# Seven block products in place of eight in a hybrid layer's mixer projections, with the value projections moved ahead and weight sums made in place

## Chip, cores and metric

The kernel runs on one core of a Trainium2 chip. The metric is device time in microseconds. Engines: PE (TensorE, matrix products), DVE (VectorE), ACT (ScalarE), POOL (GpSimd), SP (which issues nearly all transfers).

## What is computed

One step of an encoder layer on 640 tokens (512 of a prompt, 8 x 16 of samples), model width 1024, all in float32:

```python
x = x + 0.5 * swiglu(rms_norm(x), ffn1_w_in, ffn1_w_out)      # width 2816
z = rms_norm(x) @ w_in_mix     # RQ RK RV RG | FQ FK FV forget | two gates
q, k = rotary(RQ), rotary(RK)
o_ret = rms_norm(retention(q, k, RV)) * silu(RG)              # 4 heads
o_fox = forgetting_attention(norm(FQ), norm(FK), FV, forget)  # 8 heads
x = x + (sigmoid(g0) * (o_ret @ w_br_ret) + sigmoid(g1) * (o_fox @ w_br_fox)) @ w_out
x = x + 0.5 * swiglu(rms_norm(x), ffn2_w_in, ffn2_w_out)
x = x + (p @ w_ple) * sigmoid(rms_norm(x) @ w_ple_gate)
```

States, keys, values and forget logs are outputs too. Samples attend to a cache of 1024 frames.

## The kernel before

**Precision.** Each weight and activation is split in two: a high part, rounded to the matmul's fp32r format (a cast on ACT, L262 for weights), and a low part, the rest (a subtraction on DVE, L263). A product is three matmuls: high x high, high x low, low x high. `Parts` holds split weights; its tiles `wh` and `wl` have 7 slots (`NW`) of 512 columns.

**Feed-forward stages** (first one to about 470 us, second from about 1200 us). Input projections are done two column blocks at a time (gate and up, 128 columns each, `Seven`). Weights of a block are four quarters (two outputs x even and odd slices of 128 input features), the tokens two halves of 320. Seven products of sums (`ORDER`, each 4 slices x 3 matmuls of 320 columns) in three PSUM banks a, b, c replace eight plain ones. `Seven.__init__` and `split` form the sums of weights on DVE (L386 to L388, L395), partly into tiles of their own (`att`); `after` combines the banks (L413 to L421). `Norm.add_pair` makes the sums of activations (t1 to t4) in `sums` (L349 to L353), as high and low parts. Output projections go through `gemm_t`.

**The mixer** (470 to about 1088 us). A list of units, 256 weight columns each, is a feed that `run_units` turns into matmuls a few at a time: kind "n" is token-major (values, fox q and k, the last embedding product), kind "t" feature-major (retention's RQ, RK, RG, the gates, the fox output): two outputs x two halves of 320 tokens, each 8 slices x 3 matmuls into one `pg` bank, then one DVE step (`spill_t`, L753) that scales it, and a store to `zdram`. Units are loaded two ahead and split one ahead. Attention and retention run beside the feed: their steps are emitted by hand, and after each one `fill(us)` lets the feed run for so many us of the kernel's own clock (`mm` charges 320 / 2400 us for a matmul of 320 columns). The constants FILL_P0, FILL_P1 (prompt attention), FILL_S0, FILL_S (samples) and FILL_R (each of 13 steps per retention head) set how much. `defer` queues follow-up steps. `until("rv")` runs the feed as far as the values of retention, then retention starts.

Order of units before: fox v(1), q, k, v(0), q, k; RQ (2 units), RK (2), RV (4), RG (4), gates G1 (4) and G0 (4); embedding (4), fox output (4).

**Buffers.** PSUM: six `pa` banks, two `pg` banks. SBUF tiles of 640 columns: `blk` 35 slots, `att` 8, `tmp` (320 columns) 10; the tile framework orders instructions from these and from the order in which they are written. Each engine runs its queue in order.

Of the kernel before, what the change touches and what calls it, by code (L numbers as in the profile page):

```python
# [19 lines left out]
P = 128  # L20
# [26 lines left out]
FILL_P0, FILL_P1, FILL_S0, FILL_S, FILL_R, FILL_B = 1.76, 1.6, 19.8, 10.0, 3.0, 6.4  # L47
# [84 lines left out]
def kernel(  # L132
# [17 lines left out]
    NBLK, NKV, NATT, NTMP, NRAW, NW, NTINY = 35, 4, 8, 10, 2, 7, 24  # L150
# [81 lines left out]
    grows = const.tile([4 * KC, P], F32, name="grows")  # L232
# [18 lines left out]
    class Parts:  # L251
# [5 lines left out]
        def add(self, src):  # L257
            kc, n = src.shape[1], src.shape[2]
            self.per = self.per or kc
            hi = wp.tile([P, kc, n], F32R, tag="wh", name=nm("wh"), bufs=NW)  # L260
            lo = wp.tile([P, kc, n], F32R, tag="wl", name=nm("wl"), bufs=NW)
# [83 lines left out]
    def sums(ops, x0, x1, g0, g1, less):  # L345
# [8 lines left out]
        for src, names in ((d24, ("t2", "t4")), (d13, ("t1", "t3"))):  # L354
# [22 lines left out]
    class Seven:  # L377
# [5 lines left out]
        def __init__(self, raw):  # L383
            a11, a12, a21, a22 = (raw[:, o + e:o + 8:2, :] for o in (0, 8) for e in (0, 1))
# [4 lines left out]
            self.given = a11, a12, a21, a22, r1, r2  # L389
            self.banks = {}  # L390

        def split(self):
            a11, a12, a21, a22, r1, r2 = self.given
            self.w = [Parts().add(t) for t in (r2, a11, r1, a12, a21)]
            nc.vector.tensor_tensor(r1, r2, a12, op=ALU.add)  # L395
            self.w += [Parts().add(r1), Parts().add(a22)]
            return self

        def product(self, i, ops, ks=None):
            name, at = self.ORDER[i]  # L400
            w = self.w[i]
            if at not in self.banks:
                self.banks[at] = bank()
            gemm_q(self.banks[at], w, ops[name], i < 3, True, ks)
            if ks is None or ks[-1] == w.kc - 1:
                self.after(i)

        def after(self, i):
# [13 lines left out]
            elif i == 6:  # L422
                self.g, self.u = (a, c), (b, self.s5)

    class Norm:
# [23 lines left out]
        def add_sums(self, c, x0, x1):  # L449
            sums(self.ops, x0, x1, self.gain(c), self.gain(c + 1), less[:, self.n, c + 1:c + 2])  # L450
# [54 lines left out]
    def ffn(xd, norm, w_in, w_o, done, ahead=None, begun=None):  # L505
        pair0 = 0
        for npair in F_GROUPS:
# [17 lines left out]
            q = (begun or Seven(up_raw(w_in, fs[0]))).split()  # L525
            begun = None
            for f in fs:
# [16 lines left out]
                if f != fs[-1]:  # L544
                    q = Seven(up_raw(w_in, f + 1)).split()
# [125 lines left out]
    class Unit:  # L671
# [3 lines left out]
        def __init__(self, kind, src, take, done=None, begin=None, x=None):  # L675
            self.kind, self.src, self.take, self.done, self.begin = kind, src, take, done, begin
            self.x = x if x is not None else xs
            self.kc, self.n = src.shape[0] // P, src.shape[1]
            self.splits = 2 if kind == "t" else max(self.kc // 4, 1)
            self.w = [None] * self.splits  # L680

        def load(self):
            self.raw = raw_unit(self.src, self.kc, self.n)

        def split(self, i):
            ks = self.kc // self.splits
# [854 lines left out]
```

## Time and profile before

| | us |
|---|---|
| median of 3 runs | 1702.5 (1701.57 to 1702.87) |
| the profiled execution | 1700.45 |
| its span, first to last instruction | 1698.7 |
| mean granted TensorE clock | 0.998 of 2.4 GHz |

Busy time is what the profiler's rows cover. PEld is the weight load of a matmul, which runs beside PE. A row "x <-y" after a group names what ended the idle time ahead of it. Windows give busy us of each engine in a stretch, in brackets the number of instructions; the granted clock is a share of 2.4 GHz, and 0.5 is its lower level, 1.2 GHz.

### The profile page before, as it was taken

To read this page: it belongs to the slowest core of one execution; us is meant where nothing else is said; L and a number is where in the kernel's file an instruction comes from. 1 tells how busy PE (TensorE), PEld (TensorE's weight loads), DVE (VectorE), ACT (ScalarE), POOL (GpSimd) and SP (SyncE) were. 2 spreads that over 40 slices of the span, in tenths; PEclk is the share of its full clock that TensorE was granted. 3 is DMA by queue.
4 is the path that set the end of the run, shared out by engine and by line. 5 is a ranking of instruction groups with operands and counts; after the bars stand their busy time and mean duration, and the time that the engine had idled before them with its cause. 6 is when DMAs were issued, how large, how long until landed. Compare 5 with 4: busy or idle time off the path is not lost.

```text
span 1698.7 us, 30469 instructions
## 1 busy us (share of the span) xinstructions
PE 1675.4 (99%) x12264; PEld 1604.6 (94%) x12264; DVE 1081.0 (64%) x2334; ACT 693.8 (41%) x1392; POOL 1.2 (0%) x6
## 2 busy tenths in 40 slices
PE   8999999999999989999999999999999999999999
PEld 7999999999999878888899998999899999999998
DVE  6875686586776654334455555657887578558663
ACT  5552354154455433333322235434554155325442
POOL 0000000000000000000000000000000000000000
PEclk9999999999999999999999999999999999999999
DMA  7135234433632234567776469625324423533343
GB/s 238 54 119 177 74 98 140 128 90 101 203 99 82 87 104 166 204 232 242 254 228 218 154 201 337 219 83 168 90 67 147 128 83 103 172 98 97 108 136 95
DMA packets 223773, 247.35 MB, mean 146 GB/s; under 512 B 10992, under 2 KB 191120, under 8 KB 219536
## 3 DMA queue, kind: packets, MB, share of 16 engines
q1 hardware_dynamic: 223424, 245.33, 45.2%
q8 instruction: 96, 1.57, 0.4%
q14 instruction: 45, 0.37, 0.1%
q10 hardware_dynamic: 208, 0.08, 0.0%
HBM read 197.38 MB, written 47.99 MB: 144 GB/s over the span
## 4 chain that ended last, share of the span: by engine, by line
PE 90%; DMA 4%; DVE 4%; issue 1%; ACT 1%; SPq 0%; DVEq 0%
PE pa L205 63%; PE pg L205 24%; PE pa L228 4%; DMA raw<-in_ffn_w_in_dram 3%; DVE wl L263 1%; DMA out_dram<-tmp 0%; DMA blk<-zdram 0%; DMA grows<-in_norm_ple_g_dram 0%; PE pg L228 0%; DVE raw L388 0%; DVE tmp L513 0%; DVE att L395 0%; DVE pa L419 0%; DVE att L387 0%; DVE tmp L421 0%
## 5 line engine op out<-in xcount | busy, mean ns | idle before, releaser
L205 PE MATMUL pa<-blk,wh 128*128 128x320 f32 x2744 | 589.5, 310 | 2.4 <-DVE tmp L513 1.0
L262 ACT CAST wh<-raw 128x512 fp32r<-128x512 f32 (+1 forms) x436 | 265.5, 612 | 493.2 <-PE pa L205 342.4
L205 PEld LDWEIGHTS pa<-blk,wh 128*128 128x128 f32 x2744 | 454.0, 189 | 4.4 <-DVE pa L419 1.4
L205 PE MATMUL pa<-blk,wl 128*128 128x320 f32 x1372 | 399.0, 309 | 0.4 <-DVE wl L263 0.4
L263 DVE TENSOR_TENSOR wl<-raw,wh 128x512 fp32r<-128x512 f32 (+1 forms) x436 | 294.7, 678 | 94.3 <-ACT wh L262 91.2
L205 PE MATMUL pg<-blk,wh 128*128 128x320 f32 x1152 | 267.2, 318 | 1.1 <-ACT tmp L1307 0.6
L205 PE MATMUL pa<-kv,wh 128*128 128x320 f32 x1344 | 253.8, 308 | 0.0
L205 PEld LDWEIGHTS pa<-blk,wl 128*128 128x128 f32 x1372 | 252.3, 189 | 0.7 <-DVE wl L263 0.7
L205 PEld LDWEIGHTS pa<-kv,wh 128*128 128x128 f32 x1344 | 211.2, 188 | 0.0
L205 PEld LDWEIGHTS pg<-blk,wh 128*128 128x128 f32 x1152 | 191.6, 188 | 12.5 <-issue 7.6
L205 PE MATMUL pg<-blk,wl 128*128 128x320 f32 x576 | 179.1, 311 | 0.0
L205 PE MATMUL pa<-kv,wl 128*128 128x320 f32 x672 | 152.8, 307 | 0.0
L205 PE MATMUL pg<-wh,blk 128*128 128x256 f32 x768 | 149.3, 288 | 0.0
L205 PEld LDWEIGHTS pg<-wh,blk 128*128 128x128 f32 x768 | 121.1, 188 | 5.8 <-issue 3.5
L205 PEld LDWEIGHTS pa<-kv,wl 128*128 128x128 f32 x672 | 112.4, 188 | 0.0
L262 ACT CAST wh<-att 128x512 fp32r<-128x512 f32 x123 | 76.1, 619 | 86.8 <-PE pa L205 77.6
L205 PEld LDWEIGHTS pg<-blk,wl 128*128 128x128 f32 x576 | 108.3, 188 | 1.8 <-issue 1.5
L205 PE MATMUL pg<-wl,blk 128*128 128x256 f32 x384 | 108.6, 283 | 0.0
L263 DVE TENSOR_TENSOR wl<-att,wh 128x512 fp32r<-128x512 f32 x123 | 84.8, 690 | 26.9 <-ACT wh L262 26.1
L558 DVE SCALAR_TENSOR_TENSOR tmp<-pa,blk 128x320 f32<-128x320 f32 x96 | 42.6, 486 | 70.2 <-PE pa L205 69.9
L205 PE MATMUL pa<-wh,blk 128*128 128x256 f32 (+1 forms) x432 | 81.9, 285 | 0.0
L205 PEld LDWEIGHTS pg<-wl,blk 128*128 128x128 f32 x384 | 72.4, 189 | 1.6 <-issue 1.3
(246 smaller groups left out, 1967.0 us busy)
## 6 DMA issues: line engine op xcount, KB each, us to landing
raw<-in_ffn_w_in_dram SPq DMA_DIRECT2D x88, 512.0 KB, 4.1
raw<-in_w_in_mix_dram SPq DMA_DIRECT2D x25, 1024.0 KB, 5.9
raw<-in_ffn_w_out_dram SPq DMA_DIRECT2D x16, 1024.0 KB, 5.2
kv<-in_cache_fox_k_dram SPq DMA_DIRECT2D x16, 1024.0 KB, 7.4
kv<-in_cache_fox_v_dram SPq DMA_DIRECT2D x16, 1024.0 KB, 5.7
xd<-blk SPq DMA_DIRECT2D x48, 320.0 KB, 2.3
blk<-xd SPq DMA_DIRECT2D x48, 320.0 KB, 5.8
zdram<-blk SPq DMA_DIRECT2D x32, 320.0 KB, 4.2
```

The source lines that it names most:

```text
L205: i = nc.tensor.matmul(out, lhsT, rhs, start=start, stop=stop, **kw)
L228: tick(nc.tensor.transpose(out, in_, ident[: in_.shape[0], : in_.shape[0]]), 0.11)
L262: nc.scalar.copy(hi, src)
L263: nc.vector.tensor_tensor(lo, src, hi, op=ALU.subtract)
L558: nc.vector.scalar_tensor_tensor(t, ps[hf][:, :H2], 0.5, norm.rb[:, sl], op0=ALU.mult, op1=ALU.mult)
```

## The change

- The feature-major units of RQ, RK, RG, G1 and G0 (16 units) become kind "s": the two outputs of a unit are the two columns of a `Seven` (class `MixSeven`), whose banks are a from `pa`, b and c from `pg`, and whose `after` also scales by the row norm and stores two outputs to `zdram`. The fox output stays kind "t".
- The operands t1 to t4 of the mixer's activations are made by `mix_sums` in the middle of the first four units; t4 goes to DRAM (`fourth`) and comes back after the last value unit (`mix_fourth`) into the tiles of the quarter that is not needed.
- RV's four units move ahead of RQ and RK; retention starts after `until("rk")`.
- Weight sums are made in the raw tile itself, after the two quarters that are used as they are have been split (`first`); one of these can go into two `blk` tiles (`spare`). The feed-forward stages use this too.
- Slots: blk 38, tmp 8, wh and wl 6; FILL_R 2.6 for 3.0; two waits in prompt attention 1 us longer; the small tiles `cnt` and `snew` share space with others; the first norm's gains are loaded alone at the start, the other three later; each sample's fox output goes to DRAM as soon as it is made.

```diff
-FILL_P0, FILL_P1, FILL_S0, FILL_S, FILL_R, FILL_B = 1.76, 1.6, 19.8, 10.0, 3.0, 6.4
+FILL_P0, FILL_P1, FILL_S0, FILL_S, FILL_R, FILL_B = 1.76, 1.6, 19.8, 10.0, 2.6, 6.4
...
-    NBLK, NKV, NATT, NTMP, NRAW, NW, NTINY = 35, 4, 8, 10, 2, 7, 24
+    NBLK, NKV, NATT, NTMP, NRAW, NW, NTINY = 38, 4, 8, 8, 2, 6, 22
...
-    for n, g in enumerate((norm_ffn1_g, norm_mix_g, norm_ffn2_g, norm_ple_g)):
-        nc.scalar.dma_start(grows[n * KC:(n + 1) * KC, :], g[0].rearrange("(c p) -> c p", p=P))
...
+    load_gains(0, (norm_ffn1_g,))
...
+        if later:
+            later(d24[:, 1, :])
+            both = blk([P, 2, H2], F32R)
+            split_x(both[:, 0, :], both[:, 1, :], d24[:, 0, :])
+            ops["t2"].append((both[:, 0, :], both[:, 1, :]))
...
-            r1, r2 = att(shape=(P, 4, P)), att(shape=(P, 4, P))
-            nc.vector.tensor_tensor(r1, a21, a22, op=ALU.add)
-            nc.vector.tensor_tensor(r2, r1, a11, op=ALU.add)
-            nc.vector.tensor_tensor(a21, a21, a11, op=ALU.add)
...
+        def first(self, spare=False):
+            a11, a12, a21, a22 = self.given
+            self.as_is = Parts().add(a11), Parts().add(a22, spare)
+            nc.vector.tensor_tensor(a11, a21, a11, op=ALU.add)
+            nc.vector.tensor_tensor(a21, a21, a22, op=ALU.add)
+            nc.vector.tensor_tensor(a22, a11, a22, op=ALU.add)
+            return self
+        def part(self):
+            i = len(self.w)
+            if i == 0 and not hasattr(self, "as_is"):
+                self.first()
+            x11, x12, x21, x22 = self.given
+            if i == 5:
+                nc.vector.tensor_tensor(x12, x12, x22, op=ALU.add)
+            self.w.append(self.as_is[i > 1] if i in (1, 6) else Parts().add((x22, None, x21, x12, x11, x12)[i]))
...
+    def mix_fourth():
+        for j in range(KC // 2):
+            hi, lo = (part[:, H2:] for part in mix_norm.xs[2 * j])
+            t = tmp()
+            load(t, fourth[j])
+            split_x(hi, lo, t)
+            mix_norm.ops["t4"].append((hi, lo))
...
+    class MixSeven(Seven):
+        def bank(self, at):
+            return bank("pa" if at == "a" else "pg")
+        def after(self, i):
...
+            if i == 1:
+                s1, self.w1 = tmp(), tmp()
+                nc.scalar.copy(s1, a)
+                nc.vector.tensor_tensor(b, b, s1, op=ALU.subtract)
+                nc.scalar.copy(self.w1, b)
+            elif i == 2:
+                self.z1 = blk()
+                nc.scalar.copy(self.z1[:, H2:], c)
+                nc.vector.tensor_tensor(c, c, self.w1, op=ALU.subtract)
+            elif i == 3:
+                self.z0 = blk()
+                nc.vector.tensor_tensor(self.z0[:, :H2], a, r0, op=ALU.mult)
+            elif i == 4:
+                s5 = self.z1[:, H2:]
+                nc.vector.tensor_tensor(s5, b, s5, op=ALU.subtract)
+                nc.vector.tensor_tensor(s5, s5, r1, op=ALU.mult)
+            elif i == 5:
+                nc.vector.tensor_tensor(self.z0[:, H2:], c, r1, op=ALU.mult)
+                nc.sync.dma_start(zdram[self.n0], self.z0)
+            elif i == 6:
+                nc.vector.tensor_tensor(self.z1[:, :H2], b, r0, op=ALU.mult)
+                nc.sync.dma_start(zdram[self.n0 + 1], self.z1)
...
+            if u.kind == "s":
+                for i in range(7):
+                    u.split(i + 4)
+                    if nxt and i > 3:
+                        nxt.split(i - 3)
+                    for ks in ((0, 1), (2, 3)):
+                        u.seven.product(i, mix_norm.ops, ks)
+                        yield
...
-    units += units_t(Z_RQ, O_RQ, RH) + units_t(Z_RK, O_RK, RH)
+    for j in range(KC // 2):
+        units[j].middle = lambda j=j: mix_sums(j)
     units += [Unit("n", wcols(O_RV + hd * DV, DV), spill_v(hd)) for hd in range(RH)]
-    units[-1].done = lambda: ready.add("rv")
+    units[-1].done = mix_fourth
+    units += units_s(Z_RQ, O_RQ, RH) + units_s(Z_RK, O_RK, RH)
+    units[-1].done = lambda: ready.add("rk")
     for hd in range(RH):
-        units += units_t(Z_RG + 2 * hd, O_RG + hd * DV, 2)
+        units += units_s(Z_RG + 2 * hd, O_RG + hd * DV, 2)
         units[-1].done = lambda hd=hd: ready.add(("rg", hd))
-    units += units_t(Z_G1, O_ZG + D, 8) + units_t(Z_G0, O_ZG, 8)
+    units += units_s(Z_G1, O_ZG + D, 8) + units_s(Z_G0, O_ZG, 8)
...
-    until("rv")
+    until("rk")
```

## Rows read from the trace of the kernel before

**Rows 1.** The profile's totals: busy us, share of the span, instructions.

```profile
PE 1675.4 (99%) x12264; PEld 1604.6 (94%) x12264; DVE 1081.0 (64%) x2334; ACT 693.8 (41%) x1392; POOL 1.2 (0%) x6
```

**Rows 2.** Windows by stage: length, PE, PEld, DVE, ACT, POOL busy, clock, DMA share, GB/s.

```profile
200.00:284.00 84.00, 84.00 (x576) 84.00 (x575) 68.59 (x130) 46.48 (x96) 0.00 (x0) 1.00 0.34 100
470.00:530.00 60.00, 60.00 (x513) 59.95 (x512) 40.75 (x141) 33.64 (x74) 0.00 (x0) 1.00 0.34 105
530.00:660.00 130.00, 123.80 (x870) 107.06 (x869) 81.88 (x274) 53.84 (x141) 0.00 (x0) 0.99 0.30 96
660.00:858.00 198.00, 198.00 (x1907) 168.18 (x1905) 75.86 (x169) 64.19 (x142) 0.00 (x0) 1.00 0.68 233
858.00:1040.00 182.00, 181.66 (x1298) 166.70 (x1294) 103.24 (x234) 52.25 (x108) 0.00 (x0) 1.00 0.65 207
1040.00:1088.00 48.00, 47.43 (x312) 41.88 (x311) 27.63 (x66) 20.54 (x37) 0.00 (x0) 1.00 0.79 265
```

**Rows 3.** PE's waits over the whole span: us in total, times, longest.

```profile
PE pa L228 <- ACT att L997: 2.4, 1, 2.4
...
PE pa L228 <- DVE att L1001: 1.5, 1, 1.5
...
PE pa L205 <- DVE pa L419: 0.8, 2, 0.4
...
PE pg L205 <- DVE blk L753: 0.5, 1, 0.5
```

**Rows 4.** The chain of waits: start us, us, what.

```profile
931.74 3.49 PE pg L205 x24
...
1087.40 109.52 PE pa L205 x749
```

**Rows 5.** Groups by line and shape: count, busy us, mean ns, idle before them.

```profile
L263 DVE TENSOR_TENSOR wl<-raw,wh 128x512 fp32r<-128x512 f32 x416 | 285.1, 688 | 90.6 <-ACT wh L262 87.5 <-PE pg L205 0.2
...
L753 DVE TENSOR_TENSOR blk<-pg,blk 128x320 f32<-128x320 f32 x64 | 31.0, 488 | 42.4 <-PE pg L205 42.2
L386 DVE TENSOR_TENSOR att<-raw 128x512 f32<-128x512 f32 x41 | 28.4, 692 | 46.7 <-DMA raw<-in_ffn_w_in_dram 46.7
...
L285 DVE TENSOR_TENSOR blk<-att,blk 128x640 fp32r<-128x640 f32 x16 | 12.8, 822 | 0.6 <-ACT blk L284 0.2
...
L353 DVE SCALAR_TENSOR_TENSOR att<-blk,gains,att 128x320 f32<-128x320 f32 x8 | 4.4, 549 | 0.0
...
L262 ACT CAST wh<-raw 128x512 fp32r<-128x512 f32 x416 | 256.7, 619 | 470.3 <-PE pa L205 320.3 <-PE pg L205 136.2 <-DMA raw<-in_ffn_w_in_dram 4.8
```

**Rows 6.** Timeline of DVE in the first feed-forward stage: start us, us, instruction.

```profile
211.29 0.69 DVE L263 TENSOR_TENSOR wl<-att,wh 128x512 fp32r<-128x512 f32 x1
211.89 0.49 DVE L513 TENSOR_TENSOR tmp<-pa,blk 128x320 f32<-128x320 f32 x1
212.29 0.68 DVE L263 TENSOR_TENSOR wl<-raw,wh 128x512 fp32r<-128x512 f32 x1
```

**Rows 7.** Windows of line L753 alone: length, DVE busy (count), clock, DMA, GB/s.

```profile
858.00:1040.00 182.00, 17.09 (x35) 1.00 0.65 207
```

**Rows 8.** Windows of 10 us, columns as in rows 2.

```profile
560.00:570.00 10.00, 10.00 (x71) 8.84 (x70) 9.17 (x35) 3.45 (x9) 0.00 (x0) 1.00 0.16 53
...
590.00:600.00 10.00, 7.43 (x41) 5.60 (x40) 4.59 (x12) 3.06 (x7) 0.00 (x0) 1.00 0.35 107
600.00:610.00 10.00, 7.89 (x52) 5.32 (x51) 7.19 (x26) 4.55 (x13) 0.00 (x0) 0.83 0.35 115
...
1420.00:1430.00 10.00, 9.57 (x65) 9.31 (x64) 9.96 (x20) 5.94 (x14) 0.00 (x0) 1.00 0.27 79
```

**Rows 9.** Timeline of the start; in brackets the idle time before.

```profile
8.95 0.31 PE L228 MATMUL pg<-sm,grows 32*128 32x32 f32 x1 [1.96 <-DMA grows<-in_norm_ple_g_dram]
```

**Rows 10.** Retention's end: DVE's timeline, and the transfers of tile retd.

```profile
1071.93 1.28 DVE L1252 TENSOR_TENSOR blk<-blk,pa 128x512 f32<-128x512 f32 x2
...
DMA to landing us min/median/max: 2.2/5.7/7.8
```

More of the change, by code (lines that the diff above doesn't have):

```diff
@@ L343, in first_parts, with sums @@
         ops[name].append((both[:, 0, :], both[:, 1, :]))
-    def sums(ops, x0, x1, g0, g1, less):
+    def sums(ops, x0, x1, g0, g1, less, later=None):
         b12, d13, d24 = tmp(), att(shape=(P, 2, H2)), att(shape=(P, 2, H2))
@@ L381, with __init__ @@
         ORDER = (("t2", "b"), ("b11", "a"), ("t1", "c"), ("b21", "a"), ("t3", "b"), ("b22", "c"), ("t4", "b"))
-        def __init__(self, raw):
-            a11, a12, a21, a22 = (raw[:, o + e:o + 8:2, :] for o in (0, 8) for e in (0, 1))
-            r1, r2 = att(shape=(P, 4, P)), att(shape=(P, 4, P))
-            nc.vector.tensor_tensor(r1, a21, a22, op=ALU.add)
-            nc.vector.tensor_tensor(r2, r1, a11, op=ALU.add)
-            nc.vector.tensor_tensor(a21, a21, a11, op=ALU.add)
-            self.given = a11, a12, a21, a22, r1, r2
-            self.banks = {}
+        def __init__(self, a11, a12, a21, a22):
+            self.given, self.w, self.banks = (a11, a12, a21, a22), [], {}
+        def first(self, spare=False):
[13 more added lines that the diff above has]
+            self.w.append(self.as_is[i > 1] if i in (1, 6) else Parts().add((x22, None, x21, x12, x11, x12)[i]))
         def split(self):
[L393 to L396, printed above, removed]
+            if not hasattr(self, "as_is"):
+                self.first(True)
+            while len(self.w) < 7:
+                self.part()
             return self
@@ L423, in after, with quarters @@
                 self.g, self.u = (a, c), (b, self.s5)
+    def quarters(raw):
+        return (raw[:, o + e:o + 8:2, :] for o in (0, 8) for e in (0, 1))
     class Norm:
@@ L447, in add_parts, with add_sums @@
                 first_parts(self.ops, xc[:, :H2], self.gain(c), "b11")
[L449 to L450 removed]
+        def add_sums(self, c, x0, x1, later=None):
+            sums(self.ops, x0, x1, self.gain(c), self.gain(c + 1), less[:, self.n, c + 1:c + 2], later)
         def add_pair(self, x0, x1):
@@ L638 @@
     spill = dp.tile([KC, P, T], F32, name="spill")
+    mix_x = []
+    fourth = dp.tile([KC // 2, P, H2], F32, name="fourth")
     def to_mixer(xc):
@@ L682, in load, with split @@
         def load(self):
             self.raw = raw_unit(self.src, self.kc, self.n)
-        def split(self, i):
-            ks = self.kc // self.splits
-            self.w[i] = split_w(self.raw[:, :, i * P:(i + 1) * P] if self.kind == "t" else self.raw[:, i * ks:(i + 1) * ks, :])
+            if self.kind == "s":
+                self.seven = MixSeven(self.take, *(self.raw[:, e::2, o * P:(o + 1) * P] for o in (0, 1) for e in (0, 1)))
+        def split(self, upto):
+            while self.made < min(upto, self.splits):
+                i, self.made = self.made, self.made + 1
+                if self.kind == "s":
+                    self.seven.part()
+                    continue
+                ks = self.kc // self.splits
+                self.w[i] = split_w(self.raw[:, :, i * P:(i + 1) * P] if self.kind == "t" else self.raw[:, i * ks:(i + 1) * ks, :])
@@ L689, in run_units @@
     def run_units(units):
         units[0].load()
-        for i in range(units[0].splits):
-            units[0].split(i)
+        units[0].split(2)
         units[1].load()
@@ L1051, in step @@
             s, pr = n // 4, n % 4
+            if self.b == 3 and n == 2:
+                self.sr = att(shape=(P, 4, P))
+                load(self.sr.rearrange("p b m -> p (b m)"), c_sel[:, 512:])
+            elif self.b == 3 and n == 6:
+                next_sel(self.sr)
             if pr == 0:
```

125 lines of the change are left out of this document (71 added, 54 removed).

## Prediction

> **What bounds the kernel now.** I read the totals first. PE is busy 99% of the span, DVE 64%, ACT 41% [rows 1]. So the time is PE's, unless a stage says otherwise. The table by stage says it does not [rows 2]: in the mixer (470 to 1088 us) PE is busy to within 1.2% in every row but one, 530 to 660, where prompt attention leaves 6.2 us idle. DVE is what the reader should watch beside it: 82% in the feed-forward stretch 200 to 284, yet there PE loses nothing; 68%, 63%, 38% and 57% in the mixer's stretches up to 1040. PE's waits by name are few: 3.9 us on the softmax's ACT and DVE steps, and 0.5 us on the evacuation of the projections that the change rewrites [rows 3]. The chain of waits shows 24 projection matmuls in 3.49 us [rows 4], 145.4 ns each.
>
> A page of the Trainium skill, "Perfetto Trace Analysis", section Identifying the Most-Contended Engine, says that matmul busy time flatters TensorE and that weight-load busy time is the better measure. By it the mixer would have room: weight loads fill 82 to 92% of its stretches from 530 to 1040, against 100% in the feed-forward one. The rows differ from that: the projection matmul has the same pitch in both (145.4 ns in the mixer [rows 4], 84 us / 576 = 145.8 ns in the feed-forward stretch [rows 2]). So I let a removed matmul give back its whole pitch. By the page's measure, an estimate, only the mean 87% of those stretches would come back.
>
> **The sum, part by part.** The profiled execution took 1700.45 us (span 1698.7); the median of the runs is 1702.5, 2.05 us more. I work out a difference and take it from the median.
>
> *Removed matmuls.* Sixteen units of 256 columns change kind: RQ 2, RK 2, RG 4, two gates 8. A unit now has 2 outputs x 2 halves x 8 slices x 3 = 96 matmuls of 320 columns; seven products x 4 slices x 3 make 84. 16 x 12 = 192 fewer, at 145.4 ns: **-27.9 us**, if PE stays fed. The other products, attention and retention stay. (By the page's measure the same term would be 0.87 x 27.9 = 24.3 us, and the sum 3.6 us later, still inside case A below.)
>
> *DVE work of a unit.* Now 4 lo parts at 688 ns and 4 evacuations at 488 ns: 4.7 us. After: 7 lo parts, 4 weight sums (like L386, 692 ns) and 7 combining steps of 320 columns: 4.82 + 2.77 + 3.42 = 11.0 us [rows 5]. But durations overlap: a 512-wide step follows the last after 0.60 us, a 320-wide one after 0.40 us [rows 6]. So DVE is held 11 x 0.60 + 7 x 0.40 = 9.4 us by a unit, of PE's 84 x 0.1454 = 12.2 us: 77%. ACT goes from 4 to 7 casts of 619 ns plus 3 copies, under half of the unit. The cover is the same as in the feed-forward loop, whose block has the same seven parts and holds DVE for 82% with PE full [rows 2]. Alone, the unit costs PE nothing.
>
> *Beside retention.* From 858 to 1040 there are 35 evacuations, so 8.75 units [rows 7], and DVE is busy 103 of 182 us. It would gain 8.75 x (9.4 - 4.0) = 47 us while PE's stretch shrinks by 8.75 x 1.745 = 15 us: 150 of 167 us, 90%. At 92% in 560 to 570 PE lost nothing; at 99.6% in 1420 to 1430 it lost 4% [rows 8]. Bounds 0 and 4% of 167 = 7 us, both ends measured; the load is nearer the first row but the queue is less regular: **+3**. In sample attention (660 to 858) seven or eight new units stand where four and four value units stood: some 46 us more, 38% to about 61%: nothing.
>
> *Weight sums in place.* Four adds per block before, four after, in the raw tile instead of two att tiles. The lo part of a11 and of a22 now comes ahead of the first sum, about two casts and two lo parts more before the first operand. The raw tile is given up after the sixth product instead of the seventh, 1.75 us sooner. The feed-forward DVE waits for raw loads now and PE does not. **0**, bounds -1 and +1.
>
> *New operands (t1 to t4).* In each of the first four units: 4 steps at 549 ns, a 640-wide lo part (822) and a 320-wide one (like L753, 488): 3.5 us by durations, 14 in all, and a fourth part sent to DRAM and fetched back (4 loads of 160 KB, 4 splits) behind the last value unit. SP issues 8 transfers more. A store of the fourth part waits for its DVE sum, and behind it on SP stands a weight load, used a unit (14 us) later; the way back is needed by the seventh product of the first new unit, 10 us after the loads. Two POOL memsets grow by a quarter; nobody waits for them. In 470 to 530 DVE goes from 40.8 to some 54 of 60 us, 90%: covered by the same row as above. **+1**, bounds 0 and +2.4 (4% of 60).
>
> *Order and buffers.* Value projections move ahead of RQ and RK, so they lie beside prompt attention; each evacuates on ACT where a feature-major unit used DVE, which there is late, and the softmax is called for 1 us later at two points. PE idles 6.2 us in 530 to 660, and the granted clock is 0.83 in 600 to 610, right behind 590 to 600 with PE at 74% [rows 8]; part of it at the lower of the two levels, 1.2 GHz, so 0.17 x 10 = 1.7 us more are lost. Bounds: all of it back, -7.9, or half as much again, +4, since wh/wl drop from 7 to 6 and tmp from 10 to 8 and a held projection tile then holds a bank. **-1**. On SP, 20 value stores move ahead of the 8 of RQ and RK; retention starts after both either way.
>
> *End of retention.* Each of its 52 steps lets the feed run by FILL_R, cut by 0.4: 20.8 us by the kernel's own clock, where the 192 matmuls count 192 x 0.133 = 25.6. The feed runs dry 4.8 us sooner against retention's steps, and now both end together: the last head's product at 1071.9, two transfers of 5.7 us and a split, and the output projection starts at 1087.4 [rows 4, 10]. Uncovered at worst 4.8 x 0.1454 / 0.133 = 5.2 us, at best none, as six of the eight operands of the next product are there: **+3**.
>
> *Gains.* One norm's gains instead of four are loaded first. PE now waits 1.96 us for the last of them [rows 9]; the weight parts are ready only just ahead of it. Bounds -2 and 0: **-1.3**. The others come some 30 us later, three issues on ACT and one transpose.
>
> Sum: -27.9 + 3 + 0 + 1 - 1 + 3 - 1.3 = -23.2, so 1702.5 - 23.2 = **1679.3 us**. Of the best ends, -27.9 - 1 - 7.9 - 2 = -38.8 (1664); of the worst, -27.9 + 7 + 1 + 2.4 + 4 + 5.2 = -8.3 (1694).
>
> **Rivals.** *A, the forecast:* PE sets the pace, small losses; 1670 to 1688.
>
> *B, DVE or the retention chain sets the pace from 858 on.* Then what is saved in those 8.75 units (15.3 us) is lost in waits, and the rest stays: 1702.5 - 23.2 + 15.3 - 6 (the +3 and +3 already counted) = about 1689. For it: 90% on DVE, whose queue then holds both the combining steps and retention's. Against: PE full at 92% [rows 8].
>
> *C, slower: a product waits for its PSUM bank.* The units use two pg banks. A feature-major half now turns one over every 3.49 us; in the new unit bank b is read after the fifth product and written by the seventh, one product (1.75 us) later, and the next unit's first product takes c's bank one product after its last read. If DVE has a 640-wide step (822 ns), a lo part (688) and its own step (488) to do first, that is 2.0 us: late. It decides when a unit loses over 27.9 / 16 = 1.74 us. Three such hand-offs late by 0.8 us are 2.4 us a unit, 38 us: 1702.5 - 27.9 + 38 = about 1713. Against it, the feed-forward block has the same hand-off and PE waited 0.8 us for it in the whole run [rows 3]. The same page of the Trainium skill, section Optimization Strategy, says that a gap that repeats on the engine that should be saturated can mean too few buffers; that would look like this rival, and no row here shows such a gap yet.
>
> *D, it does not do what it says:* the saved products come back as waits of any kind and the time is the same; 1699 to 1706. Nothing in the profile speaks for exactly that.
>
> **How the numbers follow.** Chances: A 0.68, B 0.18, better than A (the prompt stretch gives its idle time back; 1664 to 1670) 0.04, C 0.07, D 0.03. The range holds A and B: 1669 to 1693. About 0.2% (3.4 us) is what can be told from no change: faster 0.90, same 0.03, slower 0.07.
>
> **What would show it.** Right: 192 matmuls fewer; the mixer from 470 to the output projection shorter by 20 to 26 us; DVE near 90% beside retention with PE still full; PE's waits on L414-like steps under 2 us. Wrong: PE idle repeatedly before a product on pg with the combining DVE step as releaser (C); PE idle from retention's last head to the output projection, or DVE without idle time from 858 on (B); a larger gap or a lower clock in prompt attention; the feed-forward stretches no longer full, which would mean that the sums in place or six wh/wl slots cost what I set at nothing.

## Result and profile after

| | before | after |
|---|---|---|
| median | 1702.26 us (4 runs, 1701.57 to 1702.87) | 1680.51 us (4 runs, 1678.70 to 1681.98) |
| profiled execution | 1700.45 us, span 1698.7 | 1679.24 us, span 1677.5 |
| ratio | | 0.9872, 95% interval [0.9855, 0.9889] |

The change saves 21.8 us. The forecast was 1679.3 us, and its range held the result. The totals of the changed kernel (columns as in [rows 1]):

```profile
PE 1644.2 (98%) x12073; PEld 1573.0 (94%) x12073; DVE 1177.6 (70%) x2524; ACT 740.4 (44%) x1504; POOL 1.4 (0%) x6
```

PE has 191 records fewer and is busy 31.2 us less. But its idle time grew from 1698.7 - 1675.4 = 23.3 us to 1677.5 - 1644.2 = 33.3 us, so the span shrank by 21.2. The windows by stage, the mixer's moved to where its stages now lie (columns as in [rows 2]):

```profile
200.00:284.00 84.00, 82.36 (x564) 81.83 (x563) 67.97 (x129) 43.08 (x92) 0.00 (x0) 1.00 0.34 100
470.00:530.00 60.00, 60.00 (x513) 59.82 (x512) 50.42 (x168) 35.99 (x78) 0.00 (x0) 1.00 0.34 102
530.00:660.00 130.00, 130.00 (x1017) 116.29 (x1015) 79.27 (x276) 66.43 (x170) 0.00 (x0) 1.00 0.28 90
660.00:850.00 190.00, 186.69 (x1768) 158.41 (x1767) 129.75 (x276) 82.15 (x178) 0.00 (x0) 1.00 0.73 257
850.00:1030.00 180.00, 174.65 (x1218) 155.56 (x1217) 142.56 (x316) 78.33 (x165) 0.00 (x0) 1.00 0.69 224
1030.00:1088.00 58.00, 54.72 (x372) 50.30 (x371) 31.43 (x68) 24.12 (x39) 0.00 (x0) 1.00 0.73 251
```

Read it against [rows 2]. Prompt attention (530 to 660), which left 6.2 us idle, leaves none. Every other row but 470 to 530 has lost some: 1.6 us in the feed-forward row, which was full; 3.3 in the samples; 5.4 beside retention, which had lost 0.3; 3.3 in the last row, which had lost 0.6. PE's waits by name (columns as in [rows 3]):

```profile
PE pa L205 <- ACT wh L269: 5.4, 6, 1.6
...
PE pa L228 <- DMA kv<-in_cache_fox_k_dram: 3.3, 1, 3.3
PE pa L205 <- DVE blk L1553: 2.4, 1, 2.4
PE pa L205 <- ACT blk L469: 1.8, 1, 1.8
...
PE pg L205 <- ACT tmp L1414: 1.5, 2, 1.1
...
PE pg L205 <- DVE blk L780: 0.6, 1, 0.6
...
PE pg L205 <- DVE blk L786: 0.3, 1, 0.3
PE pg L205 <- DVE blk L783: 0.3, 1, 0.3
```

L269 is the cast that makes the high part of a weight (L262 before). PE waits six times for it, each time in a feed-forward stage. L469 is a cast of the mixer's activations at 460 us. The last three rows are the bank hand-offs of the new units, 1.2 us in the whole run.

Idle time is not the whole cost, so the table sets the granted clock beside it. "Idle" is the sum over 10-us windows up to 1670 us of what PE is not busy, and "clock" the sum of (1 - granted clock) x PE's busy time, both of the profiled execution. By its mean, a window at 0.83 was a third of its time at the lower level, 1.2 GHz, and lost up to 1.7 us of work. The medians come from rounds in which the kernel before took 1702.3 to 1704.2 us, so the text compares ratios.

| kernel | median us | ratio to before, 95% interval | idle | clock |
|---|---|---|---|---|
| before | 1702.3 | | 19.2 | 2.7 |
| after | 1680.5 | 0.9872 [0.9855, 0.9889] | 29.1 | 1.4 |
| e1_eight_products | 1703.2 | 1.0000 [0.9992, 1.0009] | 19.0 | 1.7 |
| e7_eight_old_slots | 1689.8 | 0.9927 [0.9913, 0.9940] | 11.8 | 0.0 |
| e2_sums_apart | 1685.1 | 0.9897 [0.9884, 0.9910] | 27.1 | 4.9 |
| e3_sums_apart_early | 1685.9 | 0.9906 [0.9893, 0.9919] | 30.5 | 6.1 |
| e9_seven_weight_slots | 1678.5 | 0.9851 [0.9833, 0.9869] | 22.1 | 0.0 |
| e10_first_parts_in_att | 1689.0 | 0.9917 [0.9901, 0.9932] | 29.8 | 13.1 |
| e4_softmax_early | 1691.3 | 0.9936 [0.9924, 0.9948] | 33.0 | 7.5 |
| e6_before_softmax_late | 1700.8 | 0.9993 [0.9984, 1.0002] | 18.9 | 5.4 |
| e5_fill_three | 1694.0 | 0.9947 [0.9933, 0.9961] | 34.4 | 7.0 |
| e8_more_dve | 1686.0 | 0.9902 [0.9889, 0.9916] | 24.1 | 7.9 |
| e11_values_from_pool | 1688.2 | 0.9907 [0.9894, 0.9920] | 30.7 | 2.6 |
| e12_slots_and_fill | 1692.3 | 0.9935 [0.9921, 0.9949] | 36.0 | 7.7 |

The two columns don't add up to the differences. From the changed kernel to e10 they give 12.4 of 15.9 us between the profiled executions, but from it to e2 only 1.6 of 7.0. A matmul of 320 columns is recorded with some 308 ns and starts 145.4 ns after the last, so a gap of up to some 0.16 us between two starts does not show as idle time; whether such gaps are the rest is not shown.

Nor is a row a property of its kernel alone: it is one execution, in e3, e10 and e12 the slowest of its kernel (1689.9, 1695.2 and 1696.1 us). The mean clock of the kernel before ranges from 0.995 to 0.999 over 17 executions of one round, some 7 us. And from 20 to 30 us e2, e3, e8 and e10 run at 0.83 or 0.84, the others at 1.00, though e8 differs from the changed kernel only from the mixer on. So a clock loss in one profile is not yet an effect of the edit.

### The profile page after: what moved, and what is told of

Same layout as the page of the kernel before. It is cut to its first block, busy times and chain, and to the rows that moved or that the text cites. A ratio compares the mean times of both kernels' runs of the same rounds, so it can differ in the third digit from the quotient of the medians.

```text
span 1677.5 us, 30453 instructions
## 1 busy us (share of the span) xinstructions
PE 1644.2 (98%) x12073; PEld 1573.0 (94%) x12073; DVE 1177.6 (70%) x2524; ACT 740.4 (44%) x1504; POOL 1.4 (0%) x6
## 4 chain that ended last, share of the span: by engine, by line
PE 84%; DMA 8%; DVE 4%; ACT 2%; issue 1%; SPq 0%; ACTq 0%; DVEq 0%
PE pa L205 64%; PE pg L205 16%; PE pa L228 4%; DMA raw<-in_ffn_w_in_dram 3%; DMA blk<-xd 2%; DMA blk<-zdram 1%; DVE wl L270 1%; ACT wh L269 1%; DMA out_dram<-kv 1%; DMA kv<-in_cache_fox_k_dram 1%; DMA blk<-foxd 1%; DMA blk<-in_c_rope_dram 0%; PE pg L228 0%; DVE blk L592 0%; DVE kv L1268 0%
## 5 line engine op out<-in xcount | busy, mean ns | idle before, releaser
L205 PE MATMUL pa<-blk,wh 128*128 128x320 f32 x2672 | 580.1, 311 | 12.4 <-ACT wh L269 5.4
L269 ACT CAST wh<-raw 128x512 fp32r<-128x512 f32 (+1 forms) x566 | 338.3, 613 | 514.9 <-PE pa L205 334.8
L205 PEld LDWEIGHTS pa<-blk,wh 128*128 128x128 f32 x2672 | 440.6, 188 | 21.2 <-ACT wh L269 7.3
L270 DVE TENSOR_TENSOR wl<-raw,wh 128x512 fp32r<-128x512 f32 (+1 forms) x566 | 378.4, 680 | 105.8 <-ACT wh L269 100.2
L205 PE MATMUL pa<-blk,wl 128*128 128x320 f32 x1336 | 393.0, 308 | 0.0
L205 PE MATMUL pa<-kv,wh 128*128 128x320 f32 x1344 | 252.6, 308 | 0.0
L205 PEld LDWEIGHTS pa<-blk,wl 128*128 128x128 f32 x1336 | 246.7, 188 | 0.0
L205 PEld LDWEIGHTS pa<-kv,wh 128*128 128x128 f32 x1344 | 211.1, 188 | 0.0
L205 PE MATMUL pg<-blk,wh 128*128 128x320 f32 x768 | 178.4, 318 | 2.5 <-DVE blk L1430 0.9
L205 PE MATMUL pa<-kv,wl 128*128 128x320 f32 x672 | 153.8, 308 | 0.0
L205 PE MATMUL pg<-wh,blk 128*128 128x256 f32 x768 | 149.7, 290 | 1.5 <-ACT tmp L1414 1.5
L205 PEld LDWEIGHTS pg<-blk,wh 128*128 128x128 f32 x768 | 127.5, 188 | 13.3 <-issue 6.7
L205 PEld LDWEIGHTS pg<-wh,blk 128*128 128x128 f32 x768 | 120.2, 188 | 6.4 <-issue 3.0
L205 PE MATMUL pg<-blk,wl 128*128 128x320 f32 x384 | 119.2, 310 | 0.0
L205 PEld LDWEIGHTS pa<-kv,wl 128*128 128x128 f32 x672 | 112.5, 188 | 0.0
L205 PE MATMUL pg<-wl,blk 128*128 128x256 f32 x384 | 110.0, 287 | 0.0
L205 PE MATMUL pa<-wh,blk 128*128 128x256 f32 (+1 forms) x432 | 84.2, 289 | 3.2 <-ACT blk L469 1.8
L205 PE MATMUL pa<-blk,blk 128*128 128x320 f32 (+2 forms) x572 | 87.1, 300 | 0.0
L205 PEld LDWEIGHTS pa<-blk,blk 128*128 128x128 f32 (+1 forms) x572 | 77.4, 179 | 1.3 <-issue 0.6
L205 PEld LDWEIGHTS pg<-wl,blk 128*128 128x128 f32 x384 | 72.3, 189 | 2.5 <-issue 1.7
L205 PEld LDWEIGHTS pg<-blk,wl 128*128 128x128 f32 x384 | 72.2, 188 | 1.4 <-issue 1.4
```

What stands on the lines that cost most here:

```text
L205: i = nc.tensor.matmul(out, lhsT, rhs, start=start, stop=stop, **kw)
```

## The experiments

### The change taken apart: products, slots, order

Eight products in the new kernel, with FILL_R 3.0 (the old `spill_t`, which the edit puts back, is left out here):

```diff
-FILL_P0, FILL_P1, FILL_S0, FILL_S, FILL_R, FILL_B = 1.76, 1.6, 19.8, 10.0, 2.6, 6.4
+FILL_P0, FILL_P1, FILL_S0, FILL_S, FILL_R, FILL_B = 1.76, 1.6, 19.8, 10.0, 3.0, 6.4
...
-        return [Unit("s", wcols(col + n * P, 256), n0 + n) for n in range(0, count, 2)]
+        return [Unit("t", wcols(col + n * P, 256), spill_t(n0 + n)) for n in range(0, count, 2)]
...
-        units[j].middle = lambda j=j: mix_sums(j)
+        units[j].middle = None
...
-    units[-1].done = mix_fourth
```

> The 16 units go back to eight products (192 matmuls more) and the sums of activations (t1 to t4) with their trip through DRAM are left out, since nothing needs them; the new order of units, the weight sums in place, the buffers and the gains stay, and FILL_R is 3.0 again. The result is the same. Theory (a matmul is worth its whole pitch, 145.4 ns): PE is busy 27.9 us more than in the changed kernel, and the stalls that the new units brought (some 6 us of PE time beside retention, 1.8 at 460 to 470 us) are gone, so about 1680.5 + 27.9 - 8 = 1700; the prompt stretch has no idle PE, as order and timing are kept. Rival B (DVE sets the pace beside retention, so that the seven products gave only some 12 us net): about 1693 or less. Rival by weight loads: PE's own busy time rises by only some 24 us, about 1697.

And the same with the slots of before:

```diff
-    NBLK, NKV, NATT, NTMP, NRAW, NW, NTINY = 38, 4, 8, 8, 2, 6, 22
+    NBLK, NKV, NATT, NTMP, NRAW, NW, NTINY = 35, 4, 8, 10, 2, 7, 24
```

> As the kernel with eight products in the new order, but with the slots of before: 35 blk, 10 tmp, 7 wh and wl. The sums in place stay. Theory (fewer slots, not the sums in place, make PE wait at the first products of a feed-forward group and at 460 us): those waits (5.2 us for wh, 1.6 at 460, 1.5 for tmp) fall to under 2 us in all and the time falls from 1703.2 to about 1696. Rival (the longer chain of the sums in place): they stay, 1702 to 1704.

Together with the change they make a ladder, by the ratios and 1702.3 us. All but products and slots (order, softmax timing, sums in place, gains): 0.9927, **-12.4 us**. Then the new numbers of slots (wh and wl 6 for 7, tmp 8 for 10, blk 38 for 35, the small tiles 22 for 24, all at once): 0.9927 to 1.0000, **+12.4**. Then the seven products with their operands and FILL_R: 1.0000 to 0.9872, **-21.8**. The time of e1 is near what the theory expected, but for another reason: I had not seen that the rest of the change had gained 12 us and the slots had lost them. e7 beat even the better of its two expectations by 6 us.

The totals of e1 and e7:

```profile
PE 1678.2 (99%) x12265; PEld 1603.4 (94%) x12265; DVE 1084.1 (64%) x2336; ACT 687.2 (40%) x1392; POOL 1.4 (0%) x6
```

```profile
PE 1672.1 (99%) x12265; PEld 1602.8 (95%) x12265; DVE 1080.2 (64%) x2336; ACT 690.1 (41%) x1392; POOL 1.4 (0%) x6
```

From e1 to the changed kernel PE loses 192 matmuls and 34.0 us of busy time, from e7 27.9. e1 and e7 have the same matmuls, so PE's busy time of one profile is uncertain by some 6 us. Over all profiles, busy time less the clock column is on average 1672.8 us in the four kernels with eight products and 1646.4 in the ten with seven: 26.3 us for 192 matmuls, so the expected 27.9 came back nearly or wholly. Against it stand 33.3 - 23.3 = 10.0 us more idle time than in e1, so over a third of it was lost again as waits.

Where the slots cost: PE's waits in e1, and three windows of e1 (the first feed-forward stage, the second, 460 to 470 us):

```profile
PE pa L205 <- ACT wh L269: 5.2, 6, 1.7
...
PE pa L205 <- ACT blk L469: 1.6, 1, 1.6
```

```profile
200.00:460.00 260.00, 256.85 (x1756) 256.06 (x1755) 188.05 (x372) 111.07 (x223) 1.21 (x2) 1.00 0.39 119
1180.00:1660.00 480.00, 475.90 (x3294) 474.31 (x3292) 349.96 (x677) 209.74 (x411) 0.00 (x0) 1.00 0.37 114
460.00:470.00 10.00, 8.38 (x68) 8.16 (x67) 7.82 (x16) 3.53 (x6) 0.00 (x0) 1.00 0.66 211
```

The same windows of e7:

```profile
200.00:460.00 260.00, 260.00 (x1780) 260.00 (x1779) 189.32 (x375) 114.04 (x226) 1.20 (x2) 1.00 0.40 121
1180.00:1660.00 480.00, 478.56 (x3336) 477.75 (x3336) 346.50 (x677) 210.16 (x410) 0.00 (x0) 1.00 0.37 115
460.00:470.00 10.00, 9.26 (x76) 9.05 (x75) 6.70 (x14) 2.92 (x4) 0.00 (x0) 1.00 0.46 157
```

3.2 us come back in the first, 2.7 in the second, 0.9 in the third; e7 has no wait for wh among PE's waits, with the sums in place as in e1. e1 also loses 3.6 us at 930 to 950 (idle 1.95, clock 0.84) that e7 does not. e7 in turn loses 1.1 us at 1020. That explains some 9 of the 12.4; the rest is not found. These two runs don't tell the pools apart.

### Is it the sums in place after all?

The feed-forward sums in tiles of their own again (class `OldSeven`, the code of before, left out here), and the same without the last pair of lines, so that the second stage starts with the early in-place block:

```diff
-            q = (begun or Seven(*quarters(up_raw(w_in, fs[0])))).split()
+            q = (begun or OldSeven(up_raw(w_in, fs[0]))).split()
...
-                    q = Seven(*quarters(up_raw(w_in, f + 1))).split()
+                    q = OldSeven(up_raw(w_in, f + 1)).split()
...
-            begun = Seven(*quarters(up_raw(ffn2_w_in[0], 0))).first(True)
+            begun = OldSeven(up_raw(ffn2_w_in[0], 0))
```

> The changed kernel with the feed-forward stages' weight sums in tiles of their own again, as before the change; the mixer's units and all else stay. Theory (the sums in place lengthen the chain to the first operand of a group): PE's waits for the high part of a weight, 5.4 us in the changed kernel, fall to under 1 us, and the time falls by 3 to 5 us, unless the start of the second feed-forward stage loses what it gained (4 to 6 us), which would bring it back to about 1680. Rival (six slots of split weights instead of seven cause these waits): the waits stay at about 5 us and the time at 1680.5 or above.

> As the kernel with the feed-forward sums in tiles of their own, but the block with which the second feed-forward stage starts keeps the sums in place and its early split of two quarters. Theory: both gains together, 1680.5 - 4 = 1676 to 1677. Rival (the early split is worth nothing at that start): the same as the kernel with all sums apart.

Both are slower than the change, by 4.3 and 5.8 us by the ratios. PE's waits in e2:

```profile
PE pa L205 <- DVE tmp L450: 2.6, 6, 1.1
...
PE pa L205 <- ACT wh L269: 2.2, 7, 0.4
```

The waits for wh are less than half, but waits for L450, which combines banks into a tmp tile, come in their place. PE is idle 2.5 us from 200 to 460, against 3.1 in the changed kernel. With six slots the old sums wait as well, and with seven the sums in place do not (e7), so the sums in place are not the cause. Part of e2's loss is clock, which is lower in all four executions (0.996 to 0.997, against 0.997 to 0.999). In the profile the gap at 800 us is as long as in the changed kernel (3.34 against 3.31 us), but the granted clock falls here and not there, 3.2 us in two windows:

```profile
800.00:810.00 10.00, 6.66 (x51) 4.63 (x50) 4.86 (x12) 3.85 (x10) 0.00 (x0) 0.92 1.04 388
810.00:820.00 10.00, 10.00 (x89) 9.46 (x91) 5.54 (x12) 3.79 (x8) 0.00 (x0) 0.73 0.10 27
```

e3 kept the early split and still lost 2.7 us at 1210 us, with a clock of 0.83 in that window, which e2 did not. So the early split is not what shortened the second stage's start; what did is open.

Seven slots of split weights in the changed kernel:

```diff
-    NBLK, NKV, NATT, NTMP, NRAW, NW, NTINY = 38, 4, 8, 8, 2, 6, 22
+    NBLK, NKV, NATT, NTMP, NRAW, NW, NTINY = 37, 4, 8, 7, 2, 7, 22
```

> The changed kernel with 7 slots of wh and wl for 6, paid for with one slot of blk (37) and one of tmp (7). Theory (the sixth-to-seventh slot of split weights is what the feed-forward groups and the loads at 460 us lack, as with eight products): the waits for wh, 5.4 us, and for blk at 460 us, 1.8, go, and the time is 1680.5 - 7 = 1671 to 1675, as far as the smaller tmp does not cost. Rival (it was the tmp slots, 10 for 8, that made the eight-product kernel faster): no gain or slower, 1680 or above.

Two windows of e9:

```profile
200.00:460.00 260.00, 260.00 (x1782) 260.00 (x1781) 190.67 (x363) 114.30 (x228) 1.20 (x2) 1.00 0.40 122
...
850.00:1060.00 210.00, 201.85 (x1385) 178.76 (x1384) 156.81 (x358) 89.46 (x183) 0.00 (x0) 1.00 0.67 221
```

The first feed-forward stage is full again and the wait for blk at 460 us is gone (1.5 us at 480, for another tile, are new). The two pools that e9 makes smaller (blk, tmp) can't have brought that, so the slot of wh and wl is the cause there. What the seventh slot brings back is these waits; the 12.4 us above belong to all pools together. The stretch beside retention, with a tmp slot less, loses 8.2 us (6.2 in the changed kernel). Ratio 0.9851 [0.9833, 0.9869]: the intervals overlap, so it can't be told from the change, and the expected 7 us are not shown, though its lowest run, 1672.89, is the lowest of all.

The same aim by another way, the parts of one quarter in att tiles:

```diff
-                hi, lo = blk([P, kc, n], F32R), blk([P, kc, n], F32R)
+                hi, lo = spare([P, kc, n], F32R), spare([P, kc, n], F32R)
...
-            self.as_is = Parts().add(a11), Parts().add(a22, spare)
+            self.as_is = Parts().add(a11, spare and (lambda s, d: att(shape=s, dt=d))), Parts().add(a22, spare and blk)
```

> The changed kernel, where the feed-forward blocks put the split of the quarter a11 into two att tiles (those that the sums apart used before the change), so that a block takes five of the six wh and wl slots instead of six. Theory (a free slot of wh and wl at a group's start takes away the waits there): the waits for wh, 5.4 us, fall under 2 us; 1674 to 1677, the wait at 460 us may stay. Rival (the chain of the sums in place is the cause): 1680 to 1681.

The wh waits are gone (PE idle only 0.6 us from 200 to 460), but the median is 1689.0 us, 7.7 us slower by the ratios. The clock loses 13.1 us in the profile, which is the slowest execution (1695.2 us, clock 0.991); the other five have 0.993 to 0.997, the changed kernel's four 0.997 to 0.999. Two windows of e10; PE is busy throughout the second with 51 matmuls, where the changed kernel has 72 at 1.00:

```profile
1020.00:1030.00 10.00, 6.83 (x28) 3.95 (x27) 6.23 (x13) 5.83 (x9) 0.00 (x0) 0.68 1.01 339
...
1200.00:1210.00 10.00, 10.00 (x51) 10.00 (x51) 7.77 (x23) 2.83 (x6) 0.00 (x0) 0.66 0.19 53
```

Why its gaps fall where they do, and why the clock falls more often behind them, is not settled.

### Prompt attention

The softmax's two waits as before, in the changed kernel (e4, shown); and the reverse, the longer waits alone in the kernel before (e6):

```diff
-            defer(2.5, flipped)
+            defer(1.5, flipped)
...
-        defer(3.0, normed)
+        defer(2.0, normed)
```

> The changed kernel with the two waits in prompt attention as before the change (2.0 and 1.5 instead of 3.0 and 2.5). Theory (the order of the units, with evacuations on ACT instead of a late DVE, gave the prompt stretch its idle time back): PE's idle time in the prompt stretch stays under 1.5 us and the time within 1.5 us of 1680.5. Rival (the later softmax steps gave it): 4 to 7 us of idle PE come back, 1685 to 1688.

> The kernel before with nothing but the two waits of prompt attention longer by 1 us (3.0 and 2.5). Theory (the later softmax steps alone give the prompt stretch its idle time back, as the reverse edit took it away): the 6.2 us of idle PE and the 1.7 us at the lower clock go, 1702.5 - 7 = 1695 to 1697. Rival (the order of the units is needed for it as well, since a feature-major unit's evacuation on DVE is in the softmax's way): 1700 to 1703.

e4 is 10.9 us slower, but only some 4 of that lies in the prompt stretch; the rest follows later (idle 2.75 and 2.44 us at 990 and 1020 us, clock 0.87 and 0.79). The prompt windows of e4:

```profile
650.00:660.00 10.00, 8.41 (x57) 6.45 (x55) 9.35 (x26) 6.05 (x17) 0.00 (x0) 1.00 0.52 161
660.00:670.00 10.00, 9.24 (x107) 5.22 (x107) 6.78 (x25) 4.31 (x13) 0.00 (x0) 0.83 0.27 70
```

e6 gains nothing that can be told. From 530 to 660 us 5.0 of the 6.2 us of idle time are still there, nearer together and with more of the clock lost (4.1 us for 1.3), in the windows that answer to [rows 8]:

```profile
590.00:600.00 10.00, 6.60 (x27) 3.84 (x26) 4.53 (x11) 3.79 (x9) 0.00 (x0) 0.83 0.36 107
600.00:610.00 10.00, 8.68 (x50) 6.16 (x49) 6.08 (x22) 3.48 (x10) 0.00 (x0) 0.66 0.33 105
```

So neither theory stands alone. About half of the gain in this stretch came without the timing (e4 keeps everything else of the change and loses some 4 of about 7.5 us there), none that can be told with the timing alone, and a full stretch needs both. That it is the order, among what e4 keeps, is argued and not shown.

### Retention: its end, and DVE beside it

```diff
-FILL_P0, FILL_P1, FILL_S0, FILL_S, FILL_R, FILL_B = 1.76, 1.6, 19.8, 10.0, 2.6, 6.4
+FILL_P0, FILL_P1, FILL_S0, FILL_S, FILL_R, FILL_B = 1.76, 1.6, 19.8, 10.0, 3.0, 6.4
```

> The changed kernel with FILL_R 3.0 as before the change: each of retention's 52 steps lets the feed run 0.4 us longer, 20.8 us by the kernel's own clock. Theory (PE sets the pace, and the feed has to last as long as retention's steps): the feed runs dry some 20 us ahead of the last steps, which then wait for one another with PE partly idle: 5 to 15 us slower. Rival B (DVE or retention's chain sets the pace beside retention): the small stalls of 900 to 1060 us, some 6 us, go away and the time is the same or lower.

12.8 us slower by the ratios, as the theory had it. The small stalls beside retention did not go, as rival B needs: PE is idle 5.0 us from 850 to 1060, against 6.2 in the changed kernel. The end of retention in e5:

```profile
1060.00:1070.00 10.00, 5.93 (x42) 4.80 (x41) 8.29 (x28) 6.02 (x11) 0.00 (x0) 1.00 0.24 80
1070.00:1080.00 10.00, 7.85 (x51) 6.20 (x49) 5.50 (x10) 2.43 (x4) 0.00 (x0) 0.83 0.39 134
1080.00:1090.00 10.00, 8.35 (x45) 7.69 (x46) 3.96 (x7) 2.48 (x5) 0.00 (x0) 0.83 0.79 266
```

With the feed run out, the last head's steps, their transfers and the output projection's first operand follow one another in the open. The chain of waits of e5 and then of the changed kernel at that place:

```profile
1073.44 4.75 DMA blk<-retd
...
1081.58 6.04 DMA blk<-retd
1087.64 0.73 ACT blk L291
1088.42 21.61 PE pa L205 x146
```

```profile
1057.39 1.95 PE pg L205 x12
...
1061.91 20.87 PE pa L205 x142
```

In the changed kernel the chain stays on PE there until 1082.8 us.

Two low parts of every new unit computed twice:

```diff
+        def part(self):
+            super().part()
+            if len(self.w) in (3, 5):
+                src = self.given[2 if len(self.w) == 3 else 0]
+                hi, lo = self.w[-1].pieces[0]
+                nc.vector.tensor_tensor(lo, src, hi, op=ALU.subtract)
```

> The changed kernel with two low parts of every new unit computed twice: 32 DVE steps of 512 columns more, 1.2 us of DVE a unit, so 10.6 of a unit's 12.2 us, 19 us of DVE in all and some 10 beside retention. The result is the same. Theory (PE sets the pace, DVE has slack): slower by 0 to 3 us. Rival B (DVE sets the pace beside retention): slower by 8 us or more, with DVE without idle time there.

DVE is busy 18.1 us more (1195.7) and the time grows by 5.1 us by the ratios: between the two expectations. DVE does not set the pace, since some three quarters of its extra work is hidden. Three windows of e8; the first is to be read against the changed kernel's row:

```profile
850.00:1030.00 180.00, 175.32 (x1198) 153.34 (x1197) 145.92 (x319) 71.76 (x158) 0.00 (x0) 0.98 0.69 221
1020.00:1030.00 10.00, 8.47 (x36) 5.26 (x36) 4.63 (x8) 1.75 (x4) 0.00 (x0) 0.71 1.06 374
1030.00:1040.00 10.00, 10.00 (x38) 6.83 (x37) 6.64 (x17) 8.54 (x13) 0.00 (x0) 0.78 1.06 378
```

PE's idle time is no larger than without the extra steps (4.7 against 5.4 us). What the profile loses there is clock, some 2.5 us at 1020 and 2.2 at 1030. Whether the extra DVE steps brought that, or this execution, is open.

### The samples' keys

The cached values' loads moved from SP to POOL:

```diff
-                    load(t, rows[:, j:j + 4, :], 60.0)
+                    if to is self.v:
+                        nc.gpsimd.dma_start(t, rows[:, j:j + 4, :])
+                    else:
+                        load(t, rows[:, j:j + 4, :], 60.0)
```

> The changed kernel with the loads of the samples' cached values issued by POOL instead of SP. Theory (SP stands at a load of cached values, whose slot is not free, and the next sample's keys wait behind it): the wait for the keys at 797 to 807 us, 3.3 us, goes, and what the clock loses behind it; 1674 to 1678. Rival (the keys' transfer itself is late, by its slot or by the traffic): the wait stays, 1680 or above.

6.0 us slower by the ratios, not faster, with PE's wait for the keys as long as it was (3.46 us). SP's timeline in the changed kernel, and then in e11: the keys' issue hardly moves.

```profile
789.30 0.33 SPq L784 DMA_DIRECT2D zdram<-blk  x1
...
797.42 0.33 SPq L214 DMA_DIRECT2D kv<-in_cache_fox_k_dram  x1
```

```profile
788.93 0.33 SPq L784 DMA_DIRECT2D zdram<-blk  x1
...
797.06 0.33 SPq L214 DMA_DIRECT2D kv<-in_cache_fox_k_dram  x1
```

My cause was wrong. On SP the keys stand behind a new unit's store (L784, which waits 10 us for the sixth product) and a weight load. In e11 that weight load is issued at 794.50 us, and SP then stands 2.0 us at the keys for a PE product (L205), which speaks for the slot as the last thing to hold them; neither was tried alone. What made e11 slower than the change is open.

Seven slots of split weights with eight of tmp (the small tiles of 40 columns cut from 12 to 7, which is left out here), and the samples stretched:

```diff
-FILL_P0, FILL_P1, FILL_S0, FILL_S, FILL_R, FILL_B = 1.76, 1.6, 19.8, 10.0, 2.6, 6.4
+FILL_P0, FILL_P1, FILL_S0, FILL_S, FILL_R, FILL_B = 1.76, 1.6, 19.8, 10.8, 2.55, 6.4
...
-    NBLK, NKV, NATT, NTMP, NRAW, NW, NTINY = 38, 4, 8, 8, 2, 6, 22
+    NBLK, NKV, NATT, NTMP, NRAW, NW, NTINY = 37, 4, 8, 8, 2, 7, 22
```

> The changed kernel with 7 slots of wh and wl, 37 of blk and 8 of tmp (the room comes from small tiles, 7 for 12 of 40 columns), and with the samples' steps stretched: FILL_S 10.8 for 10.0, FILL_R 2.55 for 2.6, so that the feed ends where it did. Theory (the waits for wh come from the slots; the keys are late because the samples run faster than their loads): no waits for wh over 1.5 us, the wait for the keys, 3.3 us in the changed kernel and 2.0 with seven slots and 7 tmp, under 1 us; against the changed kernel 5 to 8 us less, 1672 to 1676. Rivals: the stalls beside retention (about 8 us with 7 tmp) are DVE's and ACT's order and not the tmp slots, so that they stay and grow with the denser steps: 1677 to 1680; or the wait for the keys stays at 2 us, as the transfers stretch with the samples.

Both waits that it aimed at are gone: 800 to 810 us is full, and none for wh is left in the waits. Yet its median is 1692.3 us, worse than all its expectations. PE is idle 14.2 us beside retention (850 to 1060), against 6.2 in the changed kernel and 8.2 in e9, so the rival of denser steps has its part; and retention's end came open as in e5:

```profile
1080.00:1090.00 10.00, 4.22 (x24) 3.26 (x22) 3.36 (x5) 1.97 (x3) 0.00 (x0) 1.00 0.63 196
1090.00:1100.00 10.00, 8.87 (x50) 8.87 (x51) 5.39 (x9) 8.44 (x13) 0.00 (x0) 0.83 1.05 384
```

PE is idle 10.2 us from 1060 to 1100. The balance I had set up (3 samples x 0.8 = 2.4 us more ahead of retention, 52 x 0.05 = 2.6 less beside it) was miscounted: in the code FILL_S stands for seven of the eight samples, 5.6 us, so the feed runs dry some 3 us sooner. The last store of retention's output is at 1076.0 us, against 1058.7 in the changed kernel. The run changes slots and constants at once and can't price either.

## Why the prediction was right

The mechanism of the largest term was right. That the time came out within 1.2 us was luck as well: two effects that I had put together into one term of -1 were some twelve us each in the eight-product kernels (e7, e1), with opposite signs. The changed kernel shows the same by place. Its mixer, from the first product (457.0 us before, 460.0 after) to the output projection (1087.4, 1061.9), is 28.4 us shorter, where the terms that lie in it had summed to 21.9 and the sign of being right had asked for 20 to 26. Outside it 7.2 us are lost, where I had -1.3.

- **Removed matmuls, -27.9:** right; 192 fewer against e1, to the record, and 26.3 us of busy time by the average over all profiles. That does not separate 27.9 from the 24.3 that I had set against it, but the 24.3 was misread. The Trainium skill's page "Perfetto Trace Analysis", section Identifying the Most-Contended Engine, gives weight-load busy time, beside the share of peak throughput, as a measure of how near TensorE is to its limit, and says nothing on what a removed matmul gives back. And the 87% were an average over stretches with attention in them: in the projection itself, from 931.9 to 935.0 us of the kernel before, weight loads are busy 3.10 of 3.10 us. So page and pitch agree there.
- **DVE of a unit, 0:** right. In the samples' stretch, 660 to 850 us, PE loses the 3.3 us of the keys and nothing else, with DVE at 68% (61% estimated).
- **Beside retention, +3 (0 to 7):** right in size. From 850 to 1030 PE loses 5.4 us of 180, where it had lost 0.3. DVE's busy time there grew by 43 us, near the 47 estimated, but it is at 79% and not at my 90%, as the stretch did not shrink to 167 us and holds 8 units, not 8.75. So a full DVE was not the reason. 1.5 us end with ACT (L1414) and 3.8 with DVE (L1281, L1359, L332 and the units' own hand-offs); that these steps stand behind the units' steps in their queues is argued and not shown. e8 adds 18 us of DVE and no idle time of PE there.
- **Weight sums in place, 0:** right for the sums (e2, e7), and yet the feed-forward stretch is no longer full. That is the missing seventh slot of wh and wl (e9), which I had named and put into another term.
- **New operands, +1 (0 to 2.4):** making the operands costs nothing in 470 to 530 (60.00 of 60). The 1.8 us at 460 us is in e1 too (1.6), which has no operands, and gone in e9: slots again.
- **Order and buffers, -1 (-7.9 to +4):** the step that failed, twice. The gain went to its bound: 530 to 660 has no idle PE, and e7 is 12.4 us faster than before (about 7.5 from there; in the windows 1190 to 1240 us it loses 1.4 us where the kernel before lost 4.2 and 1.4 of clock, for a reason that is open). The loss went far past its bound of +4: 12.4 by e1 and e7, with eight products. In the changed kernel the whole price of the slots was not measured; e9 shows the waits that a seventh slot of wh and wl takes away, and its time can't be told from the change. I had put "six slots for seven" and "the prompt's idle time" into one term and taken a middle; they are two mechanisms in different stages, and I had no row for either.
- **End of retention, +3 (0 to 5.2):** nothing is lost between the feed and the output projection, which starts at 1061.9 us; the 2.4 us appear one product later (L1553). The cut of FILL_R was needed: e5 puts 12.8 us on it. That it ends best at 2.6 was not tried.
- **Gains, -1.3:** wrong by its sign. The first 10 us have 6.7 us idle instead of 7.0, as the first product now waits 1.4 us for the next thing in line (ACT's blk, L348), and 1.0 us is lost between 40 and 50 us (L546), so the first 50 us lose 0.7 us more than before. That the second loss comes from the gains is not shown.

Not in the sum at all: the keys' 3.3 us. **Rival C** is out: its hand-offs took 1.2 us, not 38, and the repeating gap that would have shown it (the Trainium skill, "Perfetto Trace Analysis", section Optimization Strategy) is in no row on pg. Where such a gap did come, six waits for wh in the feed-forward stages, there was indeed a buffer too few (e9). **Rival B** is out as a pace (e8), though most of the 5.4 us end with a DVE step. The case "better than A" had its condition, the prompt's idle time, fulfilled, but not its time, as the slots, the keys and the stretch beside retention took more than the prompt gave.

## What to carry to other kernels

Price each cut in buffers as an edit of its own, in every stage that shares the pool: with eight products, the new slots cost as much as the rest of the change had gained, much of it in stages that the change was not about. When a total comes out right, undo the parts one at a time before believing the terms. Constants that make two chains end together must be set again after every edit: 0.4 us a step in e5 opened gaps of 8 us. And a clock loss in one profile has to be looked for in other executions before an edit is blamed for it.

## What was unexpected of the hardware

The granted clock doubles the price of some gaps and not of others. A gap of 3.3 us at 800 us stood beside a clock of 1.00 in the changed kernel and of 0.92 and 0.73 in e2, 3.2 us more in those two windows. Over the profiles the clock's loss runs from 0.0 us (e7, e9) to 13.1 (e10), and e10 has much the same idle time as the changed kernel (29.8 against 29.1), which loses 1.4. PE's busy time does not show it: from 1200 to 1210 us both are busy 10.00 us, with 51 matmuls at 0.66 in e10 and 72 at 1.00 in the changed kernel. What decides behind which gap the clock falls is open.
